# Seven half-size products in place of eight for 17 of the 22 w_up chunks

## The chip, the cores and the metric

The kernel runs on one core of one Trainium2 chip. The metric is device time in microseconds (us), the median of several runs. The engines are TensorE (PE in the profile; PEld is its weight load), VectorE (DVE), ScalarE (ACT), GpSimd (POOL) and SyncE (SP), which issues the DMAs. Each engine works through its own queue in order.

## The reference

One transformer-like block on 512 tokens of width 1024 in float32: a normalized input goes through four mixers (pooling, dilated attention, stick-breaking attention, S5 scan), whose gated sum is added to the input. The change lies in the feed-forward part behind them:

```python
hn = rmsnorm(x, ffn_norm_g[l])
gu = hn @ w_up[l]                                   # [512, 1024] @ [1024, 2*2816]
h = jax.nn.silu(gu[..., :FFN_HIDDEN]) * gu[..., FFN_HIDDEN:]
x = x + h @ w_down[l]                               # [512, 2816] @ [2816, 1024]
return rmsnorm(x, final_norm_g)
```

## The kernel before, in words

Activations lie transposed, features on the 128 partitions and 512 tokens in the free dimension, so width 1024 is eight tiles (k = 0 to 7). A float32 product is made of three products in the fp32r format: each operand is split into a rounded part `hi` and a remainder `lo`, and hi x hi, hi x lo and lo x hi are summed in PSUM (`mm3`, line 195; `split`, line 131: ScalarE casts, VectorE subtracts).

The weights come as a stream of chunks (`specs`, from line 138). Each is one DMA into one of two `raw` buffers (`load_next`, line 167), and is split on the chip into `hi` and `lo` buffers, two each (`split_next`, line 175), in two halves. `next_chunk` (line 186) hands out chunk c; before that it issues the load of chunk c+2 and the splitting of chunk c+1, which therefore stands on ScalarE and VectorE ahead of what chunk c's products lead to.

The feed-forward part (line 1153) runs twice over: 11 w_up chunks, then 8 w_down chunks (11 hidden tiles each); in the second part the last two w_down tiles are done by token halves (`down_half`, line 1183). One w_up chunk holds a gate tile and an up tile of 128 columns for all 1024 rows; its two products `fg` and `fu` have 24 matmuls of 512 tokens each. `glu_up` (line 1144) then multiplies both by `rb2`, the inverse norm of each token, applies silu, multiplies, and splits the result into a hidden tile. The inverse norm itself becomes known only during chunk 1, which is why `x2g`, the operand of w_up, is not normalized, and why chunk 0's `glu_up` waits for chunk 1.

The order of the instructions on each engine is that of the program text (`manual_schedule`). Side work is written as generators; `tick` (line 210) lets each active one take a step, unless a planner's clock (`_Paced`, line 65, and `_advance`, line 84: fixed cost plus cost per column) has VectorE or ScalarE more than MAX_LAG = 4.0 us behind TensorE; `finish` (line 227) takes all remaining steps at once. In the feed-forward part before the change no generator is active. PSUM has 3 banks for the main stream (`main_ps`) and 5 for side work (`side_ps`); 61 slots of [128, 512] in SBUF serve all temporary tiles.

Of the kernel before, what the change touches and what calls it, by code (L numbers as in the profile page):

```python
# [10 lines left out]
F32 = mybir.dt.float32  # L11
F32R = mybir.dt.float32r
# [7 lines left out]
P = 128  # L20
T = 512
# [22 lines left out]
CST_CNT = 512  # L44
CST_W = CST_CNT + 64

N_SLOTS = 61  # [128, 512] tiles in the rotating pool
N_RAW = 2  # weight chunks loaded ahead
N_PM = 3  # PSUM banks of the main stream; the rest serve side work
S5_RATE = 0.9  # steps of the S5 branch per tick  # L50
SB_RATE = 1.0  # steps of the stick-breaking branch per tick
MAX_LAG = 4.0  # backlog of DVE and ACT (us) at which side work pauses
H_WAIT = 4  # ticks between the S5 rotation tables and their use
SB_T = 2  # steps from stick-breaking scores to their transposes
SB_O = 2  # steps from the transposes to the outputs
DIL_O = 1  # the same for the dilated branch
N_WARM = 8  # products on constants that bring up the PE clock while the first loads run
N_HALVED = 2  # last tiles of w_down done by token halves
BC_AT = 7  # k tiles of the last product before the first half is broadcast
W0_PIECES = {0: 1, 1: 3, 4: 2, 6: 2}  # first k tile: number of k tiles, pieces of the first weight chunk  # L60
S5_PAR = 48
S5_W = S5_PAR + 4 * 256

# [25 lines left out]
def hybrid_trunk(ctx: ExitStack, tc: tile.TileContext, a: dict, out: bass.AP):  # L89
# [35 lines left out]
    def side_ps(nm):  # L125
        return pa.tile([P, T], F32, tag="at", name=nm_("s_" + nm))
# [9 lines left out]
        V.tensor_tensor(r_(lo), src, hi, ALU.subtract)  # L136
        return r_(hi), r_(lo)

    # ------------------------------------------------------- weight stream
    specs = (  # L140
        [("w_in", 17 + c, 2048) for c in range(2)]
        + [("w_in", 2 + 3 * w + g, 2048) for g in range(3) for w in range(3)]
# [6 lines left out]
        + [("w_out", n, 2048) for n in range(4)]  # L149
    )  # L150
    for part in range(2):
        specs += [("w_up", j, 2048) for j in range(NH // 2 * part, NH // 2 * (part + 1))]
        specs += [("w_down", 8 * part + n, 1408) for n in range(8)]

    class Chunk:
# [11 lines left out]
    def load_next(pieces=1):  # L167
# [4 lines left out]
            SY.dma_start(raw[:, sl], a[key][i][:, sl])  # L172
        loaded.append((raw, n))

    def split_next(pieces=2):
        raw, n = loaded[len(ready)]
        ch = Chunk()
        ch.hi = wp.tile([P, 2048], F32R, tag="hi", name=nm_("hi"))
        ch.lo = wp.tile([P, 2048], F32R, tag="lo", name=nm_("lo"))
        ready.append(ch)  # L180
        for s in range(pieces):
            sl = slice(s * n // pieces, (s + 1) * n // pieces)
            A.copy(ch.hi[:, sl], raw[:, sl])
            V.tensor_tensor(ch.lo[:, sl], raw[:, sl], ch.hi[:, sl].bitcast(F32), ALU.subtract)

    def next_chunk():
        c = used[0]
        used[0] += 1
        while len(loaded) < min(len(ready) + N_RAW, len(specs)):
            load_next()  # L190
        while len(ready) < min(c + 2, len(specs)):
            split_next()
        return ready[c]

    def mm3(ps, ch, c, nw, acts, k0=0):
# [4 lines left out]
            PE.matmul(ps, wh, al, start=False, stop=False)  # L200
            PE.matmul(ps, wl, ah, start=False, stop=k == n - 1)

    # ------------------------------------------------- side work scheduling
    active = []

    def start(gen, rate=1.0):
# [21 lines left out]
        while e in active:  # L228
            tick(True)

    # ---------------------------------------------------------------- loads
    ones = gp.tile([P, P], F32, name="ones")
    G.memset(ones, 1.0)
    warm = gp.tile([P, 1], F32, name="warm")
# [45 lines left out]
    def g3(kt):  # L280
        return cols[:, 16 + kt : 17 + kt]

    # ------------------------------------------------------------- rms norm
    def sumsq_add(acc, src):
        sq = slot("sq")
        A.activation(sq, src, AF.Square)
# [39 lines left out]
            PE.matmul(ps[:, b : b + 1], acc[:, b * P : (b + 1) * P], ones[:, 0:1], start=True, stop=True)  # L326
        return ps

    # ------------------------------------------------------------- prologue
    xg = []  # L330
    ch0 = Chunk()
    ch0.hi = wp.tile([P, 2048], F32R, tag="hi", name=nm_("hi"))
# [12 lines left out]
    rb8 = slot("rb8")  # L345
    env = {}

    # ------------------------------------------------- relative bias tables
    bias_d = dp.tile([12, BIAS_N], F32, name="bias_d")
    bias = {}  # L350

# [28 lines left out]
                SY.dma_start(bias[g, h], bass.AP(src.tensor, src.offset + off, [[1, P], [1, w]]))  # L380
            off += BIAS_L[g]

    # -------------------------------------------------------- S5 parameters
    s5 = cp.tile([P, S5_W], F32, name="s5p")
    are, aim, ldt = s5[:, 0:16], s5[:, 16:32], s5[:, 32:48]

# [287 lines left out]
            ys5.append(split(yg, "yg"))  # L674
            yield

    # ------------------------------------------------------ dilated attention
    def perm_out(t, g):
        if g == 0:
            return t  # L680
# [162 lines left out]
                    V.tensor_scalar(st[:, o : o + kn], st[:, o : o + kn], fw[g][:, b, h : h + 1], None, ALU.mult)  # L843
            yield

    # ------------------------------------------------------- stick breaking
    sq, sk, sv = [], [], []
    m_up = cst[:, CST_UP : CST_UP + P]
    m_low = cst[:, CST_LOW : CST_LOW + P]
# [44 lines left out]
                V.tensor_tensor(be[:, : n - 1], be[:, : n - 1], om[:, 1:n], ALU.mult)  # L894
            yield

    # ----------------------------------------------------------------- pool
    ypool = [None] * 4
    pwt = []

# [33 lines left out]
        V.scalar_tensor_tensor(r_(lo), ps, cols[:, 24 + g : 25 + g], hi, ALU.mult, ALU.subtract)  # L934
        ypool[g] = (r_(hi), r_(lo))

    # ------------------------------------------------------------ main: w_in
    start(bias_tables())
    start(pool_load())
    e_s5 = start(s5_gen(), S5_RATE)  # L940
# [121 lines left out]
    sb_v(1)  # L1062
    e_sb = start(sb_gen(), SB_RATE)

    # --------------------------------------------------- gates and branches
    merged = [slot("mg") for _ in range(8)]
    mg = []

# [46 lines left out]
    branch(3, yglu, last=True)  # L1115
    mixers.close()

    # ------------------------------------------------- output of the mixers
    fp = ctx.enter_context(tc.tile_pool(name="ffn", bufs=1))

    def keep(nm):
        n = nm_(nm)
        return fp.tile([P, T], F32, tag=n, name=n)

    x2, x2g = [], []
    acc = None
    for c in range(4):
# [12 lines left out]
            acc = sumsq_add(acc, t)  # L1140
    rb2 = keep("rb2")

    # ------------------------------------------------------------------ ffn
    def glu_up(psg, psu):
        tg, tu = slot("tg"), slot("tu")
        V.tensor_tensor(tg, psg, rb2, ALU.mult)
        A.activation(tg, tg, AF.Silu)
        V.tensor_tensor(tu, psu, rb2, ALU.mult)
        V.tensor_tensor(tu, tu, tg, ALU.mult)
        return split(tu, "h")  # L1150

    hk = NH // 2
    for part in range(2):
        hid = []
        for j in range(hk * part, hk * (part + 1)):
            ch = next_chunk()
            psg = main_ps("fg")
            mm3(psg, ch, 0, 256, x2g)
            if j == 1:
                bcast_rows(dgs, rb2)  # L1160
                hid.append(glu_up(*first))
            psu = side_ps("fu") if j < 2 else main_ps("fu")
            mm3(psu, ch, P, 256, x2g)
            if j == 0:
                dgs = diags(inv_rms(ssq_mm(acc)[:, 0:4], 4), "r2")
                acc = None
                first = psg, psu
                continue
            hid.append(glu_up(psg, psu))
        for nt in range(8 - N_HALVED * part):  # L1170
            ch = next_chunk()
            ps = main_ps("d")
            mm3(ps, ch, 0, P, hid)
            V.tensor_tensor(x2[nt], ps, x2[nt], ALU.add)
            if part:
                acc = sumsq_add(acc, x2[nt])

    # ------------------------- the last tiles by token halves, final rms norm
    H = T // 2
    last = [(nt, next_chunk()) for nt in range(8 - N_HALVED, 8)]  # L1180
    pq = [side_ps("ssq"), side_ps("ssq")]

# [120 lines left out]
def _layout(inp):  # L1303
    f = {k: np.asarray(v) for k, v in inp.items()}
    o = {}
    o["x"] = np.ascontiguousarray(f["x"][0].T).reshape(KT, P, T)

    def col(v, n):
        return v.reshape(n, P).T

    o["cols"] = np.ascontiguousarray(
        np.concatenate(
            [
                col(f["attn_norm_g"][0], 8),
                col(f["ffn_norm_g"][0], 8),
                col(f["final_norm_g"], 8),
                col(f["pool_scale"][0], 4),
                col(f["s5_d"][0], 4),
            ],
            axis=1,  # L1320
        )
    )
    o["cst"], o["oh"] = _constants()
    o["rel"] = f["rel_bias"]
    o["pool_w"] = np.ascontiguousarray(f["pool_w"][0].transpose(1, 0, 2).reshape(P, 512))

    def gp(v):
        return v.reshape(16, 2, 64).transpose(1, 2, 0).reshape(P, 16)

    def gpc(v):  # L1330
        return v.reshape(16, 2, 64, 16).transpose(1, 2, 0, 3).reshape(P, 256)

    ldt = np.repeat(f["s5_log_dt"][0][:, None], 64, axis=1)
    o["s5"] = np.ascontiguousarray(
        np.concatenate(
            [
                gp(f["s5_a_re"][0]),
                gp(f["s5_a_im"][0]),
                gp(ldt),
                gpc(f["s5_b_re"][0]),  # L1340
                gpc(f["s5_b_im"][0]),
                gpc(f["s5_c_re"][0].transpose(0, 2, 1)),
                gpc(f["s5_c_im"][0].transpose(0, 2, 1)),
            ],
            axis=1,
        )
    )
    o["w_in"] = _chunks(f["w_in"][0], 256)
    wb = f["w_branch"][0]
    row = 0  # L1350
    for b, kts in enumerate((4, 2, 4, 4)):
        o[f"w_g{b}"] = np.concatenate(
            [_chunks(f["w_gate"][0, b], P), _chunks(wb[row : row + kts * P], P)], axis=2
        )
        row += kts * P
    wg = f["s5_w_glu"][0].reshape(512, 2, 4, P).transpose(0, 2, 1, 3).reshape(512, 1024)
    o["w_glu"] = _chunks(wg, 512)
    o["w_out"] = _chunks(f["w_out"][0], 256)
    wu = f["w_up"][0].reshape(D, 2, NH, P).transpose(0, 2, 1, 3).reshape(D, 2 * FFN)
    o["w_up"] = _chunks(wu, 256)  # L1360
    wd = f["w_down"][0]
    o["w_down"] = np.concatenate([_chunks(wd[: FFN // 2], P), _chunks(wd[FFN // 2 :], P)])
    return o
# [19 lines left out]
```

## Time and profile before

| | |
|---|---|
| Runs | 1000.35, 1000.56, 1001.05 us; median 1000.56 |
| Profiled execution: span from first to last instruction | 999.0 us |
| TensorE busy | 986.6 us (99%), 4926 matmuls |
| VectorE busy | 574.1 us (57%) |
| ScalarE busy | 361.5 us (36%) |
| Mean granted TensorE clock | 0.995 |
| Weight loads for w_up | 22 of 1024 KB, 4.7 us from issue to landing |

The span is that of the profiled execution; the runs' times hold a little more than the span. Matmuls are pipelined, so one is recorded longer than the distance to the next; the distance between their starts is what one costs. A granted clock of 1.00 is 2.4 GHz, half of it is 1.2 GHz. All operations that go through the planner's wrapper carry one line, L79, so they are told apart by the names of their tiles.

### The profile page before, as it was taken

The numbers are of one execution on the slowest core, as the hardware profiler recorded it, in microseconds if no ns is written. First come the engines' busy times: TensorE is split into PE (matmuls) and PEld (weight loads), VectorE is DVE, ScalarE is ACT, GpSimd is POOL, SyncE is SP. The second block draws the span as 40 slices with busy tenths as digits, with TensorE's granted clock in tenths as the row PEclk, the third lists the DMA queues.
The fourth block names the chain that finished last, engine by engine and source line by source line (L and its number), as shares of the span: only waits on it lengthen the run. The fifth ranks groups of instructions, "written<-read, shape, count | busy, mean of one in ns | idle before, by whom it ended". The sixth has DMA issues, their size and how long they took to land.

```text
span 999.0 us, 12492 instructions
## 1 busy us (share of the span) xinstructions
PE 986.6 (99%) x4926; PEld 828.5 (83%) x4926; DVE 574.1 (57%) x1108; ACT 361.5 (36%) x606; POOL 4.3 (0%) x20
## 2 busy tenths in 40 slices
PE   8999999999999999999999999999999999999996
PEld 7888988988988888887888888888888888888886
DVE  6576358578877877865635565445443244454344
ACT  6253344333445444226433343332222122232231
POOL 1000000000000000000000000000000000000000
PEclk9999999999999999999999999999999999999998
DMA  7442031422112213352352323222312323222212
GB/s 270 150 139 95 9 124 52 138 73 85 64 54 69 71 49 95 119 190 92 120 176 95 117 89 125 84 85 85 114 58 99 131 85 124 87 85 87 87 59 85
DMA packets 39362, 100.18 MB, mean 100 GB/s; under 512 B 14894, under 2 KB 22747, under 8 KB 33544
## 3 DMA queue, kind: packets, MB, share of 16 engines
q1 hardware_dynamic: 39304, 99.38, 29.1%
q8 instruction: 39, 0.64, 0.2%
q14 instruction: 19, 0.16, 0.1%
HBM read 94.94 MB, written 4.42 MB: 99 GB/s over the span
## 4 chain that ended last, share of the span: by engine, by line
PE 96%; DVE 2%; ACT 1%; DMA 1%; issue 0%; SPq 0%; DVEq 0%
PE m_g L79 16%; PE m_fg L79 12%; PE m_d L79 12%; PE m_fu L79 11%; PE m_b L79 7%; PE m_qk L79 7%; PE m_v L79 5%; PE m_sqk L79 4%; PE m_o L79 4%; PE m_u L79 3%; PE m_sv L79 2%; PE s_fu L79 1%; PE m_gb L79 1%; PE m_ga L79 1%; PE s_psy L79 1%; PE s_u L79 1%
## 5 line engine op out<-in xcount | busy, mean ns | idle before, releaser
L79 DVE TENSOR_TENSOR lo<-raw,hi 128x1024 fp32r<-128x1024 f32 (+4 forms) x192 | 194.5, 1053 | 47.0 <-ACT hi L79 46.0
L79 ACT CAST hi<-raw 128x1024 fp32r<-128x1024 f32 (+4 forms) x192 | 166.1, 913 | 65.3 <-PE m_d L79 41.5
L79 PE MATMUL m_g<-xh,hi 128*128 128x512 f32 x256 | 102.6, 401 | 0.0
L79 PE MATMUL m_g<-xh,lo 128*128 128x512 f32 x256 | 100.0, 391 | 0.3 <-DVE lo L79 0.3
L79 PE MATMUL m_g<-xl,hi 128*128 128x512 f32 x256 | 99.6, 389 | 0.0
L79 PE MATMUL m_d<-hh,hi 128*128 128x512 f32 (+1 forms) x198 | 72.5, 366 | 0.0
L79 PE MATMUL m_d<-hl,hi 128*128 128x512 f32 (+1 forms) x198 | 72.4, 365 | 0.0
L79 PE MATMUL m_d<-hh,lo 128*128 128x512 f32 (+1 forms) x198 | 72.3, 365 | 0.0
L79 PE MATMUL m_fg<-x2h,hi 128*128 128x512 f32 x176 | 68.6, 390 | 0.0
L79 PE MATMUL m_fg<-x2h,lo 128*128 128x512 f32 x176 | 68.5, 389 | 0.0
L79 PE MATMUL m_fg<-x2l,hi 128*128 128x512 f32 x176 | 68.5, 389 | 0.0
L79 DVE TENSOR_TENSOR tu<-m_fu,rb 128x512 f32<-128x512 f32 x20 | 13.8, 691 | 95.0 <-PE m_fu L79 95.0
L79 PE MATMUL m_fu<-x2h,hi 128*128 128x512 f32 x160 | 62.2, 389 | 0.0
L79 PE MATMUL m_fu<-x2l,hi 128*128 128x512 f32 x160 | 62.2, 389 | 0.0
L79 PE MATMUL m_fu<-x2h,lo 128*128 128x512 f32 x160 | 62.2, 389 | 0.0
L79 ACT ACTIVATE gt<-gt 128x512 f32<-128x512 f32 x32 | 20.2, 632 | 109.1 <-DVE gt L79 109.1
L79 PEld LDWEIGHTS m_g<-xh,lo 128*128 128x128 f32 x256 | 48.0, 188 | 11.2 <-DVE lo L79 1.0
L79 PEld LDWEIGHTS m_g<-xh,hi 128*128 128x128 f32 x256 | 48.1, 188 | 10.9 <-issue 1.0
L79 PEld LDWEIGHTS m_g<-xl,hi 128*128 128x128 f32 x256 | 48.1, 188 | 10.7 <-issue 1.0
L79 ACT CAST hh<-tu 128x512 fp32r<-128x512 f32 x22 | 13.7, 622 | 113.9 <-DVE tu L79 113.9
L79 DVE TENSOR_TENSOR x<-m_d,x 128x512 f32<-128x512 f32 (+1 forms) x18 | 11.4, 632 | 65.3 <-PE m_d L79 65.3
L79 PEld LDWEIGHTS m_d<-hh,lo 128*128 128x128 f32 x198 | 37.3, 189 | 6.0
(352 smaller groups left out, 2057.6 us busy)
## 6 DMA issues: line engine op xcount, KB each, us to landing
raw<-in_w_up SPq DMA_DIRECT2D x22, 1024.0 KB, 4.7
raw<-in_w_g SPq DMA_DIRECT2D x24, 768.0 KB, 4.2
raw<-in_w_in SPq DMA_DIRECT2D x17, 1024.0 KB, 5.8
raw<-in_w_down SPq DMA_DIRECT2D x16, 704.0 KB, 4.0
raw<-in_w_g SPq DMA_DIRECT2D x8, 640.0 KB, 3.7
raw<-in_w_out SPq DMA_DIRECT2D x4, 1024.0 KB, 4.7
x<-in_x SPq DMA_DIRECT2D x8, 256.0 KB, 4.6
raw<-in_w_glu SPq DMA_DIRECT2D x2, 1024.0 KB, 7.4
```

The source lines that it names most:

```text
L79: return f(out, *args, **kw)
```

## The change

Chunks 0 to 4 stay as they are. For chunks 5 to 21 the product of a [1024 x 256] block of weights and [1024 x 512] activations is seen as a product of 2 x 2 blocks: gate and up columns, upper and lower half of k, first and second half of the tokens (256 each). Seven products of blocks, with sums of weight blocks and sums of activation blocks, replace the eight. Each block product has 4 k tiles and three matmuls per k tile, of 256 tokens.

The activation blocks (`B11`, `B21`, `B22` and four sums `T1` to `T4`) are made once by `halves_gen`, a generator of twelve steps; they are normalized, so the later `rb2` products go. The weight sums are made in `raw` by VectorE for each chunk, between the splitting of the plain blocks (into new buffers `ahi`, `alo`) and that of the sums. Within a chunk, the splitting of the next one is given out in pieces between the products (`emit`), and what follows the last product (`tail`) is issued in the next chunk. The host lays out chunks 5 to 21 in four blocks of 512 columns (`w_ups`).

```diff
+N_PLAIN = 5
...
     for part in range(2):
-        specs += [("w_up", j, 2048) for j in range(NH // 2 * part, NH // 2 * (part + 1))]
+        specs += [
+            ("w_up", j, 2048) if j < N_PLAIN else ("w_ups", j - N_PLAIN, 2048)
+            for j in range(NH // 2 * part, NH // 2 * (part + 1))
+        ]
...
+    def split_steps():
...
+        def cut(hi, lo, c0, c1):
+            def hi_():
+                A.copy(hi[:, c0:c1], raw[:, c0:c1])
+            def lo_():
+                V.tensor_tensor(lo[:, c0:c1], raw[:, c0:c1], hi[:, c0:c1].bitcast(F32), ALU.subtract)
+            return hi_, lo_
+        if not halved:
+            a0, a1 = cut(ch.hi, ch.lo, 0, n // 2)
+            b0, b1 = cut(ch.hi, ch.lo, n // 2, n)
+            return {"ha": [a0], "la": [a1], "hb": [b0], "lb": [b1]}
+        ch.ahi, ch.alo = ext["hi"](), ext["lo"]()
+        q = raw.rearrange("p (q c) -> p q c", q=4)
+        def sums():
+            V.tensor_tensor(q[:, 1::2], q[:, 3:4].to_broadcast([P, 2, 512]), q[:, 0:2][:, ::-1], ALU.add)
+            V.tensor_tensor(q[:, 0], q[:, 0], q[:, 1], ALU.add)
+            V.tensor_tensor(q[:, 2], q[:, 2], q[:, 0], ALU.add)
+        a0, a1 = cut(ch.ahi, ch.alo, 0, 1024)
+        b0, b1 = cut(ch.ahi, ch.alo, 1024, 1536)
+        c0, c1 = cut(ch.hi, ch.lo, 0, 1024)
+        d0, d1 = cut(ch.hi, ch.lo, 1024, 2048)
+        return {"ha": [a0], "la": [a1], "ha2": [b0], "la2": [b1], "sum": [sums], "hb": [c0], "lb": [c1], "hc": [d0], "lc": [d1]}
...
+    def flush(steps):
+        for n in ("ha", "la", "ha2", "la2", "sum", "hb", "lb", "hc", "lc"):
+            emit(steps, n)
...
+    def open_chunk():
+        c = used[0]
+        used[0] += 1
+        while len(loaded) < min(len(ready) + N_RAW, len(specs)):
+            load_next()
+        steps = {}
+        if len(ready) < min(c + 2, len(specs)):
+            steps = split_steps()
+        return ready[c], steps
...
         while len(ready) < min(c + 2, len(specs)):
-            split_next()
+            if specs[len(ready)][0] == "w_ups":
+                flush(split_steps())
+            else:
+                split_next()
...
+    def halves_gen():
+        def put(k, src, left, right):
+            hi, lo = split(src, "xs")
+            xs[left][k] = (hi[:, h0], lo[:, h0])
+            if right:
+                xs[right][k] = (hi[:, h1], lo[:, h1])
+        pair = None
+        for k in range(4):
+            s1, s2 = slot("xsa"), slot("xsb")
+            for t, kt in ((s1, k), (s2, k + 4)):
+                V.scalar_tensor_tensor(t, x2[kt], g2(kt), rb2, ALU.mult, ALU.mult)
+            if k % 2 == 0:
+                pair = slot("xsp")
+            A.copy(pair[:, h0 if k % 2 == 0 else h1], s1[:, h0])
+            yield
+            ta, tb = slot("xst"), slot("xsu")
+            V.tensor_tensor(ta[:, h0], s1[:, h0], s1[:, h1], ALU.subtract)
+            V.tensor_tensor(ta[:, h1], s2[:, h1], s1[:, h1], ALU.subtract)
+            V.scalar_tensor_tensor(tb[:, h0], ta[:, h0], -1.0, s2[:, h1], ALU.mult, ALU.subtract)
+            V.scalar_tensor_tensor(tb[:, h1], tb[:, h0], -1.0, s2[:, h0], ALU.mult, ALU.subtract)
+            put(k, s2, "B21", "B22")
+            yield
+            put(k, ta, "T1", "T3")
+            put(k, tb, "T2", "T4")
+            if k % 2:
+                hi, lo = split(pair, "xs")
+                xs["B11"][k - 1] = (hi[:, h0], lo[:, h0])
+                xs["B11"][k] = (hi[:, h1], lo[:, h1])
+            yield
...
+    def prod(ps, hi, lo, q, xn, first=False):
+        def mm(w, x, start=False, stop=False):
+            PE.matmul(ps, w, x, start=start, stop=stop, skip_group_check=not first)
+        for k, (ah, al) in enumerate(xs[xn]):
+            o = 512 * q + P * k
+            mm(hi[:, o : o + P], ah, start=first and k == 0)
+            mm(hi[:, o : o + P], al)
+            mm(lo[:, o : o + P], ah, stop=k == 3)
+    def up_halved(late):
+        ch, st = open_chunk()
+        pa_, pb_ = side_ps("fa"), main_ps("fb")
+        ac, b1, b2 = pa_[:, h0], pb_[:, h0], pb_[:, h1]
+        mu, cn = slot("mu"), slot("cn")
+        prod(ac, ch.ahi, ch.alo, 0, "B11", first=True)
+        emit(st, "ha")
+        late()
+        emit(st, "la")
+        A.copy(mu[:, h0], ac)
+        prod(b1, ch.ahi, ch.alo, 2, "B21", first=True)
+        emit(st, "ha2", "la2", "sum")
+        prod(ac, ch.hi, ch.lo, 0, "T2")
+        A.copy(mu[:, h1], ac)
+        prod(b2, ch.hi, ch.lo, 1, "T1", first=True)
+        A.copy(cn[:, h0], b2)
+        emit(st, "hb", "lb")
+        prod(ac, ch.hi, ch.lo, 3, "T3")
+        V.tensor_tensor(cn[:, h1], ac, cn[:, h0], ALU.add)
+        emit(st, "hc", "lc")
+        prod(b2, ch.hi, ch.lo, 2, "B22")
+        V.tensor_tensor(mu, mu, pb_, ALU.add)
+        A.activation(mu, mu, AF.Silu)
+        prod(ac, ch.ahi, ch.alo, 1, "T4")
+        def tail():
+            tu = slot("tu")
+            V.scalar_tensor_tensor(tu[:, h0], ac, -1.0, mu[:, h0], ALU.mult, ALU.mult)
+            V.scalar_tensor_tensor(tu[:, h1], cn[:, h1], -1.0, mu[:, h1], ALU.mult, ALU.mult)
+            hid.append(split(tu, "h"))
+        return tail
...
         for j in range(hk * part, hk * (part + 1)):
+            if j >= N_PLAIN:
+                if j == N_PLAIN:
+                    finish(e_halves)
+                late = up_halved(late)
+                continue
             ch = next_chunk()
             psg = main_ps("fg")
             mm3(psg, ch, 0, 256, x2g)
             if j == 1:
                 bcast_rows(dgs, rb2)
                 hid.append(glu_up(*first))
+                e_halves = start(halves_gen())
+            if j:
+                tick()
...
             hid.append(glu_up(psg, psu))
+            tick()
         for nt in range(8 - N_HALVED * part):
-            ch = next_chunk()
+            if nt == 0:
+                ch, st = open_chunk()
+                emit(st, "ha")
+                late()
+                flush(st)
+            else:
+                ch = next_chunk()
...
+    o["w_up"] = up[:N_PLAIN]
...
-    nc = _bacc.Bacc("TRN2", target_bir_lowering=False, num_devices=1)
+    nc = _bacc.Bacc("TRN2", target_bir_lowering=False, num_devices=1, dynamic_dma_scratch_size=2048)
```

## Rows read from the trace of the kernel before

**Rows 1.** The page: busy us, share, instructions; shares of the chain.

```profile
PE 986.6 (99%) x4926; PEld 828.5 (83%) x4926; DVE 574.1 (57%) x1108; ACT 361.5 (36%) x606; POOL 4.3 (0%) x20
...
PE 96%; DVE 2%; ACT 1%; DMA 1%; issue 0%; SPq 0%; DVEq 0%
```

**Rows 2.** Chain in order of time, 620 to 700 us: start, us, what.

```profile
671.03 5.44 PE m_fg L79 x24
...
681.91 5.44 PE m_fg L79 x24
```

**Rows 3.** TensorE's timeline, 970 to 984 us, narrow products: start, us, what.

```profile
971.43 0.28 PE L79 MATMUL m_d<-hh,hi 128*128 128x256 f32 x1
971.54 0.28 PE L79 MATMUL m_d<-hl,hi 128*128 128x256 f32 x1
...
983.18 0.28 PE L79 MATMUL m_d<-hh,lo 128*128 128x256 f32 x1
```

**Rows 4.** VectorE's timeline in one w_up chunk: start, us, what, idle before.

```profile
703.71 0.69 DVE L79 TENSOR_TENSOR tu<-m_fu,rb 128x512 f32<-128x512 f32 x1 [4.75 <-PE m_fu L79]
704.51 0.69 DVE L79 TENSOR_TENSOR tu<-tu,tg 128x512 f32<-128x512 f32 x1
705.89 0.69 DVE L79 TENSOR_TENSOR hl<-tu,hh 128x512 fp32r<-128x512 f32 x1 [0.69 <-ACT hh L79]
706.83 2.36 DVE L79 TENSOR_TENSOR lo<-raw,hi 128x1024 fp32r<-128x1024 f32 x2 [0.26 <-ACT hi L79]
709.15 0.69 DVE L79 TENSOR_TENSOR tg<-m_fg,rb 128x512 f32<-128x512 f32 x1
```

**Rows 5.** ScalarE's timeline in the same chunk.

```profile
705.23 0.62 ACT L79 CAST hh<-tu 128x512 fp32r<-128x512 f32 x1 [5.60 <-DVE tu L79]
705.76 2.00 ACT L79 CAST hi<-raw 128x1024 fp32r<-128x1024 f32 x2
709.88 0.63 ACT L79 ACTIVATE tg<-tg 128x512 f32<-128x512 f32 x1 [2.12 <-DVE tg L79]
```

**Rows 6.** VectorE's groups by shape: busy us, mean ns, idle before.

```profile
L79 DVE TENSOR_TENSOR lo<-raw,hi 128x1024 fp32r<-128x1024 f32 x92 | 108.5, 1220 | 39.6 <-ACT hi L79 39.1
...
L79 DVE SCALAR_TENSOR_TENSOR x2l<-x,cols,x2h 128x512 fp32r<-128x512 f32 x8 | 6.0, 752 | 6.4 <-ACT x2h L79 6.4
...
L79 DVE SCALAR_TENSOR_TENSOR pw_c<-t 64x256 f32<-64x256 f32 x8 | 3.3, 414 | 0.0
...
L79 DVE TENSOR_TENSOR t<-s5p,pwr 128x256 f32<-128x256 f32 x8 | 3.3, 415 | 0.0
```

**Rows 7.** ScalarE's groups by shape, a copy out of PSUM.

```profile
L79 ACT COPY wt<-s_wt 128x256 f32<-128x256 f32 x4 | 1.5, 385 | 0.0
```

**Rows 8.** VectorE's timeline around chunks 2 and 3.

```profile
660.19 0.69 DVE L79 TENSOR_TENSOR tu<-m_fu,rb 128x512 f32<-128x512 f32 x1 [4.75 <-PE m_fu L79]
...
671.07 0.69 DVE L79 TENSOR_TENSOR tu<-m_fu,rb 128x512 f32<-128x512 f32 x1 [4.75 <-PE m_fu L79]
...
673.25 0.69 DVE L79 TENSOR_TENSOR hl<-tu,hh 128x512 fp32r<-128x512 f32 x1 [0.69 <-ACT hh L79]
```

**Rows 9.** TensorE's timeline at the kernel's start.

```profile
6.74 0.39 PE L79 MATMUL s_u<-xh,lo 128*128 128x512 f32 x1
8.99 0.50 PE L79 MATMUL s_u<-xh,hi 128*128 128x512 f32 x1 [1.87 <-ACT hi L79]
...
11.44 0.63 PE L79 MATMUL s_u<-xh,lo 128*128 128x512 f32 x1
11.86 0.63 PE L79 MATMUL s_u<-xh,hi 128*128 128x512 f32 x1
```

**Rows 10.** Busy us by engine in stretches, then granted clock, DMA share, GB/s.

```profile
8.00:12.00 4.00, 2.93 (x7) 1.93 (x8) 3.03 (x5) 3.83 (x6) 0.00 (x0) 0.67 1.06 402
12.00:16.00 4.00, 4.00 (x18) 3.24 (x17) 3.80 (x6) 3.94 (x7) 0.00 (x0) 0.90 1.04 376
```

**Rows 11.** DMA issues on the page: count, KB each, us to landing.

```profile
raw<-in_w_up SPq DMA_DIRECT2D x22, 1024.0 KB, 4.7
```

More of the change, by code (lines that the diff above doesn't have):

```diff
@@ L173, in load_next, with emit @@
         loaded.append((raw, n))
+    ext = {}
+    def split_steps():
+        raw, n = loaded[len(ready)]
+        halved = specs[len(ready)][0] == "w_ups"
+        ch = Chunk()
+        ch.hi = wp.tile([P, 2048], F32R, tag="hi", name=nm_("hi"))
+        ch.lo = wp.tile([P, 2048], F32R, tag="lo", name=nm_("lo"))
+        ready.append(ch)
+        def cut(hi, lo, c0, c1):
[19 more added lines that the diff above has]
+        return {"ha": [a0], "la": [a1], "ha2": [b0], "la2": [b1], "sum": [sums], "hb": [c0], "lb": [c1], "hc": [d0], "lc": [d1]}
+    def emit(steps, *names):
+        for n in names:
+            for f in steps.pop(n, ()):
+                f()
+    def flush(steps):
[10 more added lines that the diff above has]
+        return ready[c], steps
     def split_next(pieces=2):
@@ L1123, in keep @@
         return fp.tile([P, T], F32, tag=n, name=n)
+    for nm in ("hi", "lo"):
+        ext[nm] = lambda nm=nm: fp.tile([P, 1536], F32R, tag="a" + nm, name=nm_("a" + nm), bufs=2)
     x2, x2g = [], []
@@ L1150, in glu_up @@
         return split(tu, "h")
+    H = T // 2
+    h0, h1 = slice(0, H), slice(H, T)
+    xs = {n: [None] * 4 for n in ("B11", "B21", "B22", "T1", "T2", "T3", "T4")}
+    def halves_gen():
[27 more added lines that the diff above has]
+            yield
@@ L1154, in hybrid_trunk @@
         hid = []
+        late = lambda: None
         for j in range(hk * part, hk * (part + 1)):
+            if j >= N_PLAIN:
[3 more added lines that the diff above has]
+                continue
             ch = next_chunk()
@@ L1176, in hybrid_trunk @@
                 acc = sumsq_add(acc, x2[nt])
-    H = T // 2
     last = [(nt, next_chunk()) for nt in range(8 - N_HALVED, 8)]
@@ L1359, in _layout @@
     wu = f["w_up"][0].reshape(D, 2, NH, P).transpose(0, 2, 1, 3).reshape(D, 2 * FFN)
-    o["w_up"] = _chunks(wu, 256)
+    up = _chunks(wu, 256)
+    o["w_up"] = up[:N_PLAIN]
+    hv = up[N_PLAIN:].reshape(NH - N_PLAIN, P, 2, 4, 2, P).transpose(0, 1, 4, 2, 3, 5)
+    o["w_ups"] = np.ascontiguousarray(
+        np.stack([hv[:, :, 0, 0], hv[:, :, 1, 1], hv[:, :, 0, 1], hv[:, :, 1, 0]], axis=2)
+    ).reshape(NH - N_PLAIN, P, 2048)
     wd = f["w_down"][0]
```

## The prediction

> **What bounds the kernel now.** The page comes first: TensorE is busy for 986.6 of the span's 999.0 us and the chain that ended last is 96% TensorE, while VectorE is busy 57% [rows 1]. So shorter TensorE work shortens the kernel wherever nothing else becomes late. The chain in order of time shows the stage that changes: the first product of chunk 4 starts at 671.03 and that of chunk 5 at 681.91, so a w_up chunk takes 10.88 us with no gap, 0.2267 us for each of its 48 products of 512 tokens [rows 2]. The next view is TensorE's timeline near the end, where products of 256 tokens already stand: 99 of them start from 971.43 to 983.18, one every 0.1199 us, a little over half of 0.2267 [rows 3]. The last views are VectorE's and ScalarE's timelines in a chunk: VectorE waits 4.75 us before it can use the second product [rows 4, 5, 8]. That idle time is what the change spends.
>
> **TensorE, per halved chunk.** 48 x 0.2267 = 10.88 us go; 7 x 4 x 3 = 84 products of 256 tokens come, 84 x 0.1199 = 10.07 us. That is 0.81 us less, 13.8 us over 17 chunks. The saving is far below one in eight, because the narrow product costs 53% of the wide one. At exactly half, 0.1133, it would be 1.36 us a chunk; I take 0.1199, whose rows have the same shapes and a weight load each.
>
> **VectorE, per halved chunk.** Durations: 1.22 us for 1024 columns, 0.415 for 256 even where an operand is a broadcast view, 0.414 for a two-step operation with a constant [rows 6], 0.69 for 512 [rows 4]. Two independent operations overlap by 0.07: two of 1024 take 2.36 together, and the third starts 2.32 after the first. So the steps are 1.15, 0.61 and 0.34 us. One that reads its predecessor's result starts 0.11 after that one's end (703.71 + 0.69 to 704.51); handing over to ScalarE or back costs 0.03 to 0.04 [rows 4, 5]. The sums of 1024 columns with block-reversed and broadcast operands have no row of that size: between 1.22 (as plain) and 1.38 (two of 512); I take 1.22.
>
> In queue order, from the first of the tail's two multiplications (t = 0): second multiplication 0.34, its end 0.75, ScalarE's cast of the hidden tile (0.62 and two handovers) 1.44, its remainder; `la` at 2.05; `la2` 3.20; first sum 3.81; second sum 5.14, ends 5.83; third sum behind it to 6.62. `hb` waits for the second sum and takes 1.05 on ScalarE, so `lb` starts at 6.95, not at 6.55. The `cn` addition follows at 8.10, `lc` 8.44, `mu` addition 9.59 to 10.28, silu (0.63 and handovers) to 10.98. The next chunk's multiplications need that silu and stand ahead of everything else in the queue. So VectorE's round is about 11.0 us, some 0.15 us **more** than a whole chunk took before, though its busy time is only about 9.6. ScalarE has 3 casts of 1.05, two of 0.62, three PSUM copies of 0.385 and one silu of 0.63, 6.2 us [rows 5, 7]; it is no bound.
>
> TensorE feels this at its seventh product: `T4` overwrites the PSUM half that `cn` reads, so it waits for `cn`, at t + 8.5. Behind it stand all products of the next chunk. In the first halved chunk of a part VectorE has no tail to do and in the last of a part the chunk split ahead is a smaller w_down one, so chunks 5, 10, 11 and 21 run at 10.07; chunks 6 and 12 start with VectorE 0.3 late, about 10.35; the other 11 run at 11.03. Sum: 4 x -0.81 + 2 x -0.53 + 11 x 0.15 = **-2.6 us**, not -13.8. Bounds of the round: 10.07 (TensorE's own) to 11.6 (no overlap, a rival below), or -13.8 to +5.
>
> **The start of chunk 5.** `halves_gen` has twelve steps (A, B, C for four k). A is two two-step operations of 0.75 [rows 6], step about 0.67, so 1.3; B four half operations, two of them dependent, and a remainder, 2.1; C two remainders (three for odd k), 1.2 or 1.8. In all 20 us. They are given out by two ticks a chunk from chunk 1 on, eight ticks. The planner's own clock (0.09 us + 1.04 ns a column) has a lag of 5.7 at the first tick of chunk 4, because the first halved chunk has just been split, and skips that one; so seven steps come by ticks and five by `finish`, all of them ahead of chunk 5. Chunk 2 and 3 have room for their steps: VectorE's 4.75 us of waiting [rows 8]. From the end of chunk 3's remainder at 673.94 VectorE then works without a break: step 6, 1.8; the split of chunk 5, 7.3 (1.15 + 0.61 + 1.33 + 0.69 + 1.12 + 1.15 + 1.22); the gate and up operations of chunk 4, 3.4 (0.61 + 0.80 + 0.69 + 0.69 + 0.61); steps 7 to 12, 1.3 + 2.1 + 1.2 + 1.3 + 2.1 + 2.3 (the last waits for ScalarE's three casts). That is 22.8 us, to 696.7. TensorE reaches chunk 5 at 681.91; six products of `B11` need only k 0 and 1 (0.72), then the last remainder is missing: **14.1 us idle**. Bounds: 10 if VectorE also uses up the 2.7 us that it leaves free before chunks 2 and 3's second products and the tail of C is hidden, 16 if each operation takes its whole duration.
>
> **The clock after that.** At the kernel's start TensorE stood still from 7.1 to 8.99 and then products of 512 started 0.42 us apart (11.44 to 11.86) [rows 9]; the granted clock was 0.67 in 8 to 12 us and 0.90 in 12 to 16, so at 1.2 GHz for 2.6 + 0.8 us, in which about half the work was lost [rows 10]. I take one such spell: **+1.6 us** (0 to 3.4). After it VectorE has caught up.
>
> **At nothing.** Chunks keep their 1 MB, land in 4.7 us, and are asked for a chunk ahead [rows 11]; the load waits longer for its buffer (`lc` is its last reader), but nothing is queued on SP behind it that anybody needs within a chunk. If that cover went, 4.7 us once. A PSUM copy of 0.385 lies beside a whole product group of 1.44. The first w_down chunk of a part needs the late hidden tile only at its last k, 30 products in. The smaller descriptor scratch and the removed comments move no instruction.
>
> **Sum.** The profiled execution has 999.0 us of span, 1.6 less than the runs' median of 1000.56; I leave that distance as it is. -2.6 + 14.1 + 1.6 = +13.1: **1013.6 us**.
>
> **Rivals.** *TensorE stays the bound in the halved chunks* (some of VectorE's waits overlap better than I string them). Then all 17 save 0.81: -13.8 + 14.1 + 1.6 = +1.9, 1002.5. For it: VectorE's busy time, 9.6, is below 10.07. Against it: hb, the hidden tile's cast and silu are each waits that rows 4 and 5 show whole.
>
> *Faster: a dense stream of VectorE operations runs shorter than its rows.* No row shows more than three independent ones in a run. Were their steps 15% shorter, the round would be under 10.07 (-13.8), the 22.8 us at chunk 5 would be 19.4 and the idle 10.7: -13.8 + 10.7 + 1.6 = -1.5, 999. It decides from the point where the idle and its clock fall below 13.8 with the round below TensorE's. Against it: the three in rows 4 keep 1.15.
>
> *No overlap.* VectorE starts each operation only at the end of the one before. The round gains seven overlaps of 0.07 to 0.08, 11.55; 11 x 0.52 is 5.7 us more, and some 25 operations at chunk 5 give 2 us: 1021. The Trainium skill, VectorE: DVE Perf Modes, "The DRAIN you can't avoid", says that the next operation waits until the pipe is empty; by that, this would be the time. The trace disagrees where the second has no wait (2.36 for two of 1.22).
>
> *The clock falls again and again.* TensorE now idles about 1 us in each of 11 chunks; at 1.6 us each that is +17.6, 1031. The Trainium skill, TensorE: Matmul & The Clock Gate, "A second HAM failure mode", tells of such short idles between groups. For it: 1.9 us of idle was enough at the start [rows 9, 10]; against it: there the products before had been few, here TensorE is over 90% busy.
>
> **Chances.** Forecast 0.50 (own range 1008 to 1018); TensorE-bound 0.18 (1000 to 1006); faster 0.12; no overlap 0.10; clock 0.10. Leaving out the faster case and most of the clock case gives 1001 to 1024. A measurement of this kernel tells 0.2%, 2 us, from no change. Faster is the third rival and a little of the first, 0.14; same is about half of the first, 0.09; slower the rest, 0.77.
>
> **What would show it.** A TensorE gap of 10 to 16 us behind six narrow products of `fb` or `fa` at the first halved chunk, released by VectorE's remainder of `xs`; a low granted clock for some 3 us behind it; narrow products every 0.120 us; in the middle halved chunks a gap of about 1 us before the seventh group, released by `cn`, and 11.0 us from chunk to chunk. It is wrong if the gap at chunk 5 is under 8 us, or the middle chunks take 10.1.

## The result and the profile after

| | before | after |
|---|---|---|
| Median of the runs | 1000.70 us | 1014.29 us (1013.50 to 1015.44) |
| Span of the profiled execution | 999.0 us | 1011.7 us |
| TensorE busy | 986.6 us | 979.2 us |
| VectorE busy | 574.1 us | 659.7 us |

The median before is that of four runs, one more than in the table ahead of the change. The ratio is 1.014, 95% interval 1.0126 to 1.0154: the change makes the kernel 1.4% slower, 13.6 us. TensorE does have less to do, and the chain shows where the time went. These are the busy line and the chain by engine on the page after, against [rows 1]:

```profile
PE 979.2 (97%) x5538; PEld 849.2 (84%) x5538; DVE 659.7 (65%) x1248; ACT 412.9 (41%) x709; POOL 4.3 (0%) x20
...
PE 79%; DVE 14%; ACT 5%; issue 1%; DMA 1%; SPq 0%; DVEq 0%; ACTq 0%
```

TensorE's share of the chain fell from 96% to 79%; VectorE now carries 14%. The starts of the product groups in TensorE's timeline give a ledger by stage:

| stage | before, us | after, us | difference |
|---|---|---|---|
| up to the first w_up product | 625.5 | 624.4 | -1.1 |
| chunks 0 to 4 | 56.28 | 56.28 | 0.0 |
| chunks 5 to 10 | 65.28 | 79.55 | +14.3 |
| w_down, first part | 59.84 | 59.87 | 0.0 |
| chunks 11 to 21 | 119.68 | 118.70 | -1.0 |
| the rest | 72.4 | 72.9 | +0.4 |

The first line isn't the change's: the instructions up to there are the same, and over the profiled executions of all kernels told of here that product starts anywhere from 624.0 to 627.5; what moves it, no run here asks. The last line isn't the change's either: over the same executions it takes 72.4 to 73.1. Between the two, from the first w_up product to the second part's first w_down product, it takes 314.4 us instead of 301.1. These 13.3 us are the change's, and the forecast's +13.1 is best held against them.

The start of chunk 5 in TensorE's timeline (start, us, what, idle time before):

```profile
680.69 0.28 PE L80 MATMUL s_fa<-xsh,ahi 128*128 128x256 f32 x1
...
681.28 0.28 PE L80 MATMUL s_fa<-xsh,alo 128*128 128x256 f32 x1
693.96 0.58 PE L80 MATMUL s_fa<-xsh,ahi 128*128 128x256 f32 x1 [12.39 <-ACT xsh L80]
695.14 0.58 PE L80 MATMUL s_fa<-xsl,ahi 128*128 128x256 f32 x1 [0.60 <-DVE xsl L80]
695.52 0.41 PE L80 MATMUL s_fa<-xsh,alo 128*128 128x256 f32 x1
695.73 0.41 PE L80 MATMUL s_fa<-xsh,ahi 128*128 128x256 f32 x1
...
698.93 0.29 PE L80 MATMUL s_fa<-xsh,hi 128*128 128x256 f32 x1
699.06 0.29 PE L80 MATMUL s_fa<-xsl,hi 128*128 128x256 f32 x1
```

Six products run on k 0 and 1, then TensorE stands for 12.4 us until ScalarE has cast the last pair, and for 0.6 more until VectorE has its remainder. Behind that the products start 0.21 us apart instead of 0.12, up to 698.9. The second group starts at 696.37; the first alone would have taken 1.44, so 14.2 us are lost before it, 0.4 of them by four products that ran 0.21 apart without a wait (695.52 to 696.37); and it takes 2.56 instead of 1.44, 1.1 more. The granted clock in stretches (us of each engine, then the clock, DMA share, GB/s) says why:

```profile
684.00:688.00 4.00, 0.00 (x0) 0.00 (x0) 3.37 (x8) 2.21 (x4) 0.00 (x0) 0.66 0.51 215
688.00:692.00 4.00, 0.00 (x0) 0.00 (x0) 4.00 (x9) 1.67 (x4) 0.00 (x0) 0.50 0.00 0
692.00:696.00 4.00, 1.44 (x5) 1.15 (x6) 3.97 (x7) 2.68 (x4) 0.00 (x0) 0.50 0.00 0
696.00:700.00 4.00, 4.00 (x24) 4.00 (x24) 2.65 (x4) 0.89 (x2) 0.00 (x0) 0.63 0.00 0
700.00:704.00 4.00, 4.00 (x36) 4.00 (x35) 1.41 (x3) 2.36 (x4) 0.00 (x0) 1.00 0.00 0
```

While TensorE stood (0 products from 684 to 692) the clock fell to 0.50, 1.2 GHz, and from 688 to 692 VectorE was busy for the whole 4.00 us.

One round of VectorE in a steady halved chunk, from one first multiplication of the tail to the next (to be read against [rows 4]):

```profile
707.41 0.42 DVE L80 SCALAR_TENSOR_TENSOR tu<-s_fa,mu 128x256 f32<-128x256 f32 x1 [0.76 <-ACT mu L80]
707.75 0.41 DVE L80 SCALAR_TENSOR_TENSOR tu<-cn,mu 128x256 f32<-128x256 f32 x1
708.87 0.69 DVE L80 TENSOR_TENSOR hl<-tu,hh 128x512 fp32r<-128x512 f32 x1 [0.70 <-ACT hh L80]
709.48 1.82 DVE L80 TENSOR_TENSOR alo<-raw,ahi 128x1024 fp32r<-128x1024 f32 x2
711.22 2.67 DVE L80 TENSOR_TENSOR raw<-raw 128x1024 f32<-128x1024 f32 x3
714.27 1.23 DVE L80 TENSOR_TENSOR lo<-raw,hi 128x1024 fp32r<-128x1024 f32 x1 [0.39 <-ACT hi L80]
715.42 0.42 DVE L80 TENSOR_TENSOR cn<-s_fa,cn 128x256 f32<-128x256 f32 x1
715.75 1.22 DVE L80 TENSOR_TENSOR lo<-raw,hi 128x1024 fp32r<-128x1024 f32 x1
716.88 0.68 DVE L80 TENSOR_TENSOR mu<-mu,m_fb 128x512 f32<-128x512 f32 x1
718.32 0.43 DVE L80 SCALAR_TENSOR_TENSOR tu<-s_fa,mu 128x256 f32<-128x256 f32 x1 [0.76 <-ACT mu L80]
```

The round is 718.32 - 707.41 = 10.91 us, with three waits for ScalarE: 0.70, 0.39 and 0.76. TensorE's seventh product of that chunk:

```profile
715.04 0.28 PE L80 MATMUL m_fb<-xsh,lo 128*128 128x256 f32 x1
715.89 0.39 PE L80 MATMUL s_fa<-xsh,ahi 128*128 128x256 f32 x1 [0.57 <-DVE cn L80]
716.11 0.28 PE L80 MATMUL s_fa<-xsl,ahi 128*128 128x256 f32 x1
```

It waits until `cn` is done (715.42 + 0.42). Counted between starts, 0.73 us are lost before it (0.85 instead of 0.12) and 0.10 behind it (0.22 instead of 0.12): 10.08 becomes 10.91 us from chunk to chunk, against 10.88 before [rows 2]. TensorE's waits in total (engine, what it waited for, us, times, longest):

```profile
PE s_fa L80 <- ACT xsh L80: 12.4, 1, 12.4
PE s_fa L80 <- DVE cn L80: 7.4, 13, 0.6
```

### The profile page after: what moved, and what is told of

Read it like the earlier page. It is cut to its first block, busy times and chain, and to the rows that moved or that the text cites. A ratio compares the mean times of both kernels' runs of the same rounds, so it can differ in the third digit from the quotient of the medians.

```text
span 1011.7 us, 13943 instructions
## 1 busy us (share of the span) xinstructions
PE 979.2 (97%) x5538; PEld 849.2 (84%) x5538; DVE 659.7 (65%) x1248; ACT 412.9 (41%) x709; POOL 4.3 (0%) x20
## 4 chain that ended last, share of the span: by engine, by line
PE 79%; DVE 14%; ACT 5%; issue 1%; DMA 1%; SPq 0%; DVEq 0%; ACTq 0%
PE m_g L80 16%; PE m_d L80 12%; PE m_b L80 7%; PE m_qk L80 7%; PE m_v L80 4%; PE m_sqk L80 4%; PE m_o L80 4%; DVE lo L80 4%; PE m_u L80 3%; DVE raw L80 3%; DVE alo L80 2%; PE m_sv L80 2%; PE m_fg L80 2%; PE s_fa L80 2%; ACT hi L80 2%; PE m_fb L80 2%
## 5 line engine op out<-in xcount | busy, mean ns | idle before, releaser
L80 PE MATMUL m_d<-hl,hi 128*128 128x512 f32 (+1 forms) x198 | 72.4, 366 | 0.0
L80 PE MATMUL s_fa<-xsh,ahi 128*128 128x256 f32 x136 | 40.4, 297 | 20.1 <-ACT xsh L80 12.4
L80 PEld LDWEIGHTS s_fa<-xsh,ahi 128*128 128x128 f32 x136 | 26.2, 193 | 23.4 <-ACT xsh L80 12.6
L80 DVE TENSOR_TENSOR raw<-raw 128x512 f32<-128x512 f32 (+1 forms) x51 | 44.2, 867 | 1.2
L80 PEld LDWEIGHTS m_d<-hh,hi 128*128 128x128 f32 x198 | 37.4, 189 | 6.0
L80 PEld LDWEIGHTS m_d<-hl,hi 128*128 128x128 f32 x198 | 37.4, 189 | 5.9
L80 DVE TENSOR_TENSOR gt<-m_b,gt 128x512 f32<-128x512 f32 x24 | 16.5, 689 | 38.0 <-PE m_b L80 32.8
L80 PE MATMUL s_fa<-xsl,ahi 128*128 128x256 f32 x136 | 38.9, 286 | 0.6 <-DVE xsl L80 0.6
L80 PE MATMUL s_fa<-xsh,alo 128*128 128x256 f32 x136 | 38.7, 285 | 0.0
```

The costliest lines, as they stand in the source:

```text
L80: return f(out, *args, **kw)
```

## The experiments

All stand against the kernel before, in ratios with 95% intervals; chunk times are distances between the starts of a chunk's seventh product and the next chunk's.

**Seven plain chunks (e1).** Does the idle at the first halved chunk have the size of VectorE's backlog?

```diff
-N_PLAIN = 5
+N_PLAIN = 7
```

> Seven plain chunks instead of five, so chunks 7 to 21 are halved. VectorE-backlog theory: the twelve steps of halves_gen get two more chunks of cover, so from the same step costs VectorE ends its last remainder about 8 us (not 13) after TensorE needs it: idle at the first halved chunk 7 to 9 us instead of 12.4 + 0.6, about 1008 us. The two chunks that go back to plain cost nothing (10.88 against 10.91). Rival, the idle time is a fixed cost of the first halved chunk (its weights, buffers, loads): 12 to 13 us remain, 1014.

Measured: 1008.95 us, ratio 1.008 (1.0063 to 1.0096). The idle is 6.8 + 0.6 us, as expected of the backlog:

```profile
PE s_fa L80 <- ACT xsh L80: 6.8, 1, 6.8
```

The low clock came here too (the second group takes 2.51 us instead of 1.44).

**No weight sums (e2).** Is it VectorE that holds the steady chunks?

```diff
-        emit(st, "ha2", "la2", "sum")
+        emit(st, "ha2", "la2")
+        st.pop("sum", None)
```

(and the same in `flush`)

> The three VectorE sums of weight blocks are left out (the blocks are used as loaded), everything else stays. VectorE-round theory: VectorE's round falls below TensorE's, so the 13 chunks that take 10.91 us take 10.08 (-10.8 us), the 0.57 us gaps before the seventh product vanish, and the split ahead of chunk 5 is about 3 us shorter, so the idle there falls from 13.0 to about 10: about 1000 us. Rival, the gaps are a cost of the narrow products themselves or of ScalarE's copies: chunks stay at 10.9, 1011 to 1014.

Measured: 1005.81 us, ratio 1.0046 (1.0031 to 1.0061). The idle at chunk 5 fell to 9.5 + 0.6 us as expected. But the steady chunks take 10.46 us, not 10.08: VectorE's round was a limit, and something stands close behind it. ScalarE and VectorE around the sixth product of a steady chunk:

```profile
732.76 0.37 ACT L80 COPY cn<-m_fb 128x256 f32<-128x256 f32 x1 [1.07 <-PE m_fb L80]
733.03 2.00 ACT L80 CAST hi<-raw 128x1024 fp32r<-128x1024 f32 x2
734.11 1.23 DVE L80 TENSOR_TENSOR lo<-raw,hi 128x1024 fp32r<-128x1024 f32 x1 [2.53 <-ACT hi L80]
735.26 0.42 DVE L80 TENSOR_TENSOR cn<-s_fa,cn 128x256 f32<-128x256 f32 x1
```

VectorE idles for 2.53 us, so its work is no limit here. Its queue is: `cn` stands behind `lb`, `lb` waits for `hb`, and `hb` stands on ScalarE behind the copy that waits for TensorE's fourth product. The seventh product waits for `cn` and comes 0.3 late, although VectorE has just stood idle.

**`cn` ahead of `lb` (e3).** Order alone.

```diff
-        emit(st, "hb", "lb")
+        emit(st, "hb")
         prod(ac, ch.hi, ch.lo, 3, "T3")
         V.tensor_tensor(cn[:, h1], ac, cn[:, h0], ALU.add)
+        emit(st, "lb")
```

> In VectorE's queue the cn addition stands ahead of lb, into the time in which lb waits for ScalarE. Nothing else moves. VectorE-round theory: the gap before the seventh product goes or shrinks, but VectorE still does the same work in a round, only its wait of about 0.3 us is filled, so the steady chunks take 10.6 to 10.7 us and TensorE waits elsewhere: about 1010 us. Rival, it is only the place of cn behind lb that holds TensorE up: steady chunks at 10.08, about 1003.

Measured: 1009.79 us, ratio 1.0084 (1.0069 to 1.0099); steady chunks 10.58 us. The gap before the seventh product is gone, and the wait has moved to the third, which needs ScalarE's first copy of `mu`:

```profile
PE s_fa L80 <- ACT mu L80: 3.2, 13, 0.3
```

So the place of `cn` gave what filling a 0.3 us wait gives, and no more: VectorE's round, with the waits that are left in it, is the limit.

**No activation sums (e4).** `halves_gen` returns at once, and the products read halves of `x2g`.

```diff
+        for k in range(4):
+            (ah, al), (bh, bl) = x2g[k], x2g[k + 4]
+            for n in ("B11", "T1", "T2"):
+                xs[n][k] = (ah[:, h0], al[:, h0])
+            for n in ("B21", "B22", "T3", "T4"):
+                xs[n][k] = (bh[:, h1], bl[:, h1])
+        return
```

> The activation sums are left out: halves_gen does nothing and the seven products read halves of x2g as it stands. VectorE-backlog theory: the idle at chunk 5 and the low clock behind it go (-14.2 and -1.1 us), the steady chunks stay at 10.91: about 999 us. Rival, the wait at chunk 5 comes from the split of its weights ahead of it: most of it stays, over 1008.

Measured: 1000.36 us, ratio 0.9992 (0.9983 to 1.0002). The waits of 12.4 and 0.6 us are gone: chunk 5's first two groups start at 680.29 and 681.72, 1.43 apart, and the granted clock stays at 1.00. The steady chunks still take 10.91. A short wait of another kind is left before the third product:

```profile
683.90 0.39 PE L80 MATMUL s_fa<-x2h,hi 128*128 128x256 f32 x1 [0.58 <-ACT mu L80]
```

It is for ScalarE's first copy of `mu`, which stands in its queue behind the cast of chunk 4's hidden tile and a cast of weights. The split of chunk 5's weights, which this kernel still does in the same place, does not by itself make chunk 5 wait for 13 us. It counts as work that stands ahead of the last six steps, as e2 showed: without the sums the wait was 2.9 us shorter.

**No weight sums, `cn` first (e5).** The edits of e2 and e3 together.

> The weight sums are left out as in e2 and the cn addition stands ahead of lb as in e3. Theory: two limits lie one behind the other. VectorE's round (10.91 us, 10.58 with its wait filled) is the first; with the sums gone the second is the queue order: cn stands behind lb, lb behind ScalarE's hb, hb behind the copy after the fourth product (10.46 in e2). With both gone TensorE is the bound: steady chunks 10.08, no gap before the seventh product, about 1000 us. Rival, 10.46 is what narrow products with their restarts cost in a chunk: 10.4 to 10.5 again, 1005.

Measured: 1006.75 us, ratio 1.0046 (1.0032 to 1.006); steady chunks 10.48. The number is that of the rival, but its reason is not: the gap has moved to the third product. The chain in order of time through one chunk (start, us, what):

```profile
745.34 0.42 DVE cn L80
745.76 2.27 DVE lo L80 x2
748.03 0.61 DVE mu L80
...
748.72 0.64 ACT mu L80
...
749.38 0.77 DVE tu L80 x2
...
750.17 0.62 ACT hh L80
750.79 0.28 ACT mu L80
...
751.12 1.70 PE s_fa L80 x12
752.82 1.44 PE m_fb L80 x12
754.26 1.44 PE s_fa L80 x12
```

It is a ring: `cn`, both `lo`, the `mu` addition, silu, the tail, the cast of the hidden tile, ScalarE's `mu` copy behind it, and the third, fourth and fifth product, which ends where the next `cn` starts. It has no sums in it. The `mu` addition needs neither `lo`; it only stands behind them.

**Order alone (e6).** Nothing left out: `cn` ahead of `lb`, and the `mu` addition ahead of `lc`.

```diff
-        emit(st, "hb", "lb")
+        emit(st, "hb")
         prod(ac, ch.hi, ch.lo, 3, "T3")
         V.tensor_tensor(cn[:, h1], ac, cn[:, h0], ALU.add)
-        emit(st, "hc", "lc")
+        emit(st, "lb", "hc")
         prod(b2, ch.hi, ch.lo, 2, "B22")
         V.tensor_tensor(mu, mu, pb_, ALU.add)
+        emit(st, "lc")
```

> Order alone, nothing left out: cn ahead of lb, and the mu addition ahead of lc, so that lc fills VectorE's wait for silu (0.76 us). Theory: VectorE's round falls from 10.58 (e3) to about 9.9, below TensorE's 10.08, so steady chunks take 10.1 us and the idle at chunk 5 stays 13: about 1003 us. Rival, VectorE's work as such is the bound and waits cannot be filled (a dense stream runs no faster): 10.5 to 10.6 as in e3, 1009.

Measured: 1003.38 us, ratio 1.0019 (1.001 to 1.0029). Steady chunks take 10.08 us, and TensorE waits nowhere in them. VectorE around the sixth product:

```profile
735.21 0.42 DVE L80 TENSOR_TENSOR cn<-s_fa,cn 128x256 f32<-128x256 f32 x1 [0.42 <-ACT hi L80]
735.55 1.22 DVE L80 TENSOR_TENSOR lo<-raw,hi 128x1024 fp32r<-128x1024 f32 x1
736.68 0.68 DVE L80 TENSOR_TENSOR mu<-mu,m_fb 128x512 f32<-128x512 f32 x1
737.28 1.22 DVE L80 TENSOR_TENSOR lo<-raw,hi 128x1024 fp32r<-128x1024 f32 x1
...
738.41 0.42 DVE L80 SCALAR_TENSOR_TENSOR tu<-s_fa,mu 128x256 f32<-128x256 f32 x1
```

`lc` (737.28) now fills the wait for silu. One steady chunk of this kernel in a stretch (TensorE, its weight loads, VectorE, ScalarE):

```profile
726.30:736.38 10.08, 10.08 (x87) 10.08 (x85) 8.91 (x13) 5.72 (x9) 0.00 (x0) 1.00 0.32 106
```

and of the changed kernel:

```profile
726.80:737.71 10.91, 10.34 (x84) 10.14 (x84) 8.99 (x13) 5.62 (x9) 0.00 (x0) 1.00 0.30 98
```

The same instructions (13 in either stretch) keep VectorE busy for 8.9 to 9.0 us in both. What made 10.91 was not the work but the waits strung between it.

**Order and more plain chunks (e7, e8).** The edit of e6 with `N_PLAIN = 8` (e7) and 7 (e8).

> The order of e6 and eight plain chunks, so chunks 8 to 21 are halved. Theory: the twelve steps and the first split are done by VectorE some 2 us after TensorE reaches chunk 8, mostly behind products that do not need them; no low clock. 14 chunks at 10.1 instead of 10.88 are 11 us less than before, 1 to 3 us are lost at the start: 991 us. Rival, the start costs its 13 us or the halved chunks stay at 10.6 or more: 997 or above.

Measured: 995.09 us, ratio 0.9933 (0.9918 to 0.9948), 0.7% faster than the kernel before and faster than the changed one. The halved chunks take 10.08; at chunk 8 one wait is left, and the granted clock around it stays at 1.00 (the stretch from 720 to 722 us):

```profile
721.60 0.39 PE L80 MATMUL s_fa<-xsh,hi 128*128 128x256 f32 x1 [2.18 <-ACT mu L80]
720.00:722.00 2.00, 0.40 (x3) 0.40 (x4) 1.38 (x2) 2.00 (x4) 0.00 (x0) 1.00 0.85 360
```

TensorE no longer waits for the twelve steps: VectorE starts their last remainder at 709.70, and chunk 8 begins at 716.39. The wait is the one that e4 left, for ScalarE's first `mu` copy behind the cast of the last plain chunk's hidden tile. It is 1.6 us longer than there; the last step, 1.8 us of VectorE's queue, stands ahead of what leads to that cast.

From the first w_up product to the second part's first w_down product it takes 292.3 us where the kernel before takes 301.1, 8.8 less: 14 x 0.80 = 11.2 less the start of chunk 8, 2.4. The runs show 6.4 less, and in the profiled one w_up is reached 2.0 us later (at 627.5) and the end takes 0.7 longer. The 991 that was expected reckoned with neither.

> The same with seven plain chunks. Theory: the idle of e1 at chunk 7 (about 7 us, with a short spell of low clock) stays, and 15 halved chunks save 12 us: 996 to 998. Rival: the order of the halved chunks also shortens the idle, 992 or below.

Measured: 1000.64 us in one run, with 6.8 + 0.6 us of idle at chunk 7 as in e1, and 10.08 a chunk. Its time is above the 996 to 998 expected, for two reasons. The w_up stage started late (626.8). And the start of chunk 7 costs 10.5 us, more than the 7 us of idle and the short spell of low clock that were expected: its first three groups take 8.6, 1.1 and 0.8 us longer than 1.44 each, the second and most of the third at half clock, so that only 1.5 of the 12 us saved are left. What was asked, whether the order shortens the idle, is answered by the idle: it does not.

## Why the prediction was right

Forecast 1013.6 us, measured 1014.29. The steps, one by one:

- *A narrow product costs 0.1199 us, a chunk without waits 10.07.* 10.08 in e6 and e7, where nothing waits.
- *VectorE's round, about 11.0.* Measured 10.91. From its first operation the forecast put `la` at 2.05, the sums at 3.81, `lb` at 6.95, `cn` at 8.10, `lc` at 8.44, the `mu` addition at 9.59; the trace has 2.07, 3.81, 6.86, 8.01, 8.34 and 9.47. The 0.1 us from `lb` on are the dependent sums: the three, 1.22 + 0.69 + 0.69 long, take 2.67 together, so each starts some 0.03 after the sum that it reads has ended, where the forecast took 0.11 from [rows 4]. The sums with broadcast and reversed operands cost what plain ones do (1.22 us for 1024 columns):

```profile
L80 DVE TENSOR_TENSOR raw<-raw 128x1024 f32<-128x1024 f32 x17 | 20.7, 1218 | 0.0
```

- *The seventh product waits for `cn`.* It does, 13 times, and costs 0.73 + 0.10 us each time, where about 1 was forecast.
- *The halved chunks together, -2.6 us.* Measured -1.1 - 1.0 = -2.1 (part 0's chunks 5 to 10 are 14.3 longer, of which 14.2 + 1.1 are the start). The first halved chunk of a part was forecast without a wait and the second with one of 0.3. Both were late: chunks 5 and 11 lost 0.4 each, and chunks 6 and 12 already take 10.9. The reason that e2 showed, `cn` behind `lb` behind ScalarE's copy, holds without any lag of VectorE and was missing in the forecast; in e3, where `cn` stands ahead of `lb`, chunk 11 loses nothing. That the sum of the chunks came out only 0.5 off is in part luck: these four chunks cost 1.9 more than forecast, and the other eleven steady ones, at 10.91 instead of 11.03, 1.3 less.
- *The start of chunk 5, 14.1 us.* Measured 14.2 up to the second group, or 13.9 without the 0.4 that is the clock's. VectorE's last remainder was forecast for 696.7 with the first w_up product at 625.5, so for 695.6 here; it ended at 695.1. e1 (7.4 us of idle with two more chunks of cover) and e4 (none of it without the activation sums) show that it is this backlog.
- *The clock, 1.6 us.* Measured 1.5: one whole group of twelve ran at half clock (1.1), and before it four products that did not wait (0.4).

The sum was right because each term was; the chunks came out 0.5 us dearer than forecast, the start and the clock 0.3 cheaper, so 13.3 instead of 13.1. That the median lies only 0.7 us from the forecast says little more: its own runs spread over 1.9.

The rivals: *TensorE stays the bound* did not come true, as VectorE's three waits stand whole in the trace. But its argument, a busy time below 10.07, was sound (9.0 measured; the 9.6 counted overlaps twice), and e6 shows that the 10.08 is there for another order of the same instructions. *A dense stream runs shorter* is refuted by the densest stretch after, the remainders at chunk 5:

```profile
692.60 0.68 DVE L80 TENSOR_TENSOR xsl<-xsb,xsh 128x512 fp32r<-128x512 f32 x1
693.20 0.68 DVE L80 TENSOR_TENSOR xsl<-xst,xsh 128x512 fp32r<-128x512 f32 x1
693.80 0.68 DVE L80 TENSOR_TENSOR xsl<-xsu,xsh 128x512 fp32r<-128x512 f32 x1
```

One starts every 0.60 us, as the forecast took from [rows 4] (0.61). The same rows refute *no overlap*: each starts 0.08 before the last has ended. The Trainium skill (VectorE: DVE Perf Modes, "The DRAIN you can't avoid") says that the next operation starts only when the pipe is empty, but adds that one that is not held starts earlier. The prediction took only the first half; in these rows the next operation does start earlier. *The clock falls again and again* did not happen: the granted clock is 1.00 from 712 to 760 us with a gap of 0.57 us in each chunk. What the Trainium skill (TensorE: Matmul & The Clock Gate, "A second HAM failure mode") tells of short idles between groups is not seen at this size.

## What to carry to other kernels

When products are traded for sums, the engine that makes the sums need not be full to become the limit: string its queue out over one round with its waits, and compare that with the bound engine's round; here 9.0 us of work took 10.9, and moving two instructions made it 10.1. One-time work that the new form needs must be done before its first use, and "spread over the chunks before" has to be counted in that engine's free microseconds, not in ticks. A long stop of TensorE costs more than its length, since the first products behind it run at half clock (here 1.5 us on top of 13.0).

## What the runs showed of the hardware

- The first product behind one of the 13 waits for `cn` costs 0.10 us more than its neighbours (0.22 to the next start instead of 0.12), 1.3 us in all beside the waits' length.
- An idle of 2.18 us in the middle of a busy stretch (e7) left the granted clock at 1.00, although at the kernel's start 1.87 us stood before a fall [rows 9, 10]; what sets the two apart, no run here shows. After 12.4 us (the changed kernel) and 6.8 us (e1) of idle it was down, at 0.50.
